# Hybrid decoder block: the bias of the softmax exponentials computed by VectorE instead of ScalarE

## Chip, cores and metric

One core of a Trainium2 chip. The metric is the device time of one launch in microseconds. Below, PE is TensorE, PEld its weight loads, DVE is VectorE, ACT is ScalarE, POOL is GpSimd, and SP is SyncE, which here only issues DMAs.

## What is computed

One decoder block on x of 1 x 2048 x 1024 in float32. The block normalises x, multiplies by a 1024 x 8192 input matrix, runs two branches, merges them by gates and ends with an output projection. One branch is a gated linear recurrence. The other, in which the change lies, is causal attention with 8 heads, each with two softmaxes whose difference weighs the values:

```
for qb in range(S // 128):                       # 16 query tiles of 128 rows
    s = einsum('bqhcd,bkhcd->bhcqk', q[q0:q1], k[:q1]) * HEAD_DIM ** -0.5      # c = 0, 1
    s = where(causal mask, s, -inf)
    p = softmax(s, axis=-1)
    w = p[:, :, 0] - lam * p[:, :, 1]
    outs.append(einsum('bhqk,bkhe->bqhe', w, v[:q1]))
o = rmsnorm(concatenate(outs), subln_g) * (1 - lam_init)
```

## The kernel before

Matrix operands are kept as a pair of float16 numbers (a high and a low part), and each product is three matmuls. The program has four stages: input transposes and first projections, the recurrence with its projections (to about 500 us), attention (about 500 to 1960 us), and the output stage.

Attention is written as 128 units, one for each head h and query tile t, with t from 0 to 15 inside a head. A unit goes through these steps:

- `a_scores`: score matmuls (L812) into the PSUM tile `sc`, of which there are two buffers. DVE copies them into the SBUF tiles `e0` and `e1` (one for each softmax) and takes row maxima into `mx` (L820; L824 for the 128 columns on the diagonal).
- `a_exp`: DVE reduces `mx` to `rm` (L835, 128 x 2, one column for each softmax). The bias `nb = -scale * rm + lsp` is 128 x 2 as well (L838). ACT then takes the exponentials of `e0` and `e1` in place (L848) with a column of `nb` as bias. Their sums go to `sm` for t of 8 and more, where a row has two pieces and so four exponentials, and directly to the chunk's tile `s0` for smaller t.
- `a_comb`, for the unit before: DVE adds the sums (L856), forms the factor `rs` (L858, L859) and combines both softmaxes (L865). ACT rounds the result to float16 (L867), POOL forms the low part (L868), and four or two transposing DMAs on SP write `pt` (L871).
- `a_pv`, three units late: the product with V (L888). Every fourth unit ends with `a_norm`: squares on ACT (L900), a chain of small DVE operations that reads `s0` (L902 to L909, L120 to L126), and the results `y`.

Between units, "fill" work is placed: the projections of the next head (k, q, v with za) and the gates gm. One fill is 24 or 48 matmuls (L192, L696) into the PSUM tile `mm` with two buffers, which ACT empties (for a gate: tanh, L713). Its weights are loaded by SP (L145, tile `wst`, two buffers, 512 KB each), squared and summed by ACT (L156, tile `jk`), rounded by DVE (`w_s`, L158), summed over partitions by PE (`tot`, L162), and scaled to float16 by ACT (L177) and DVE (L178).

The steps of a unit are written in the order `"0fc1eFp"`: scores, a fill, the combination of the unit before, further scores, exponentials, more fills, the product with V. That is not the final order. The tile framework schedules the written program with a timeline of its own, so an instruction's place on its engine's queue follows from its plan. On the chip each queue runs strictly in that order, and an instruction that waits holds up all that stands behind it.

Of the kernel before, what the change touches and what calls it, by code (L numbers as in the profile page):

```python
# [14 lines left out]
AF = mybir.ActivationFunctionType  # L15
ALU = mybir.AluOpType
# [32 lines left out]
def kernel(  # L49
# [23 lines left out]
    nc = tc.nc  # L73
# [20 lines left out]
    with ExitStack():  # L94
# [102 lines left out]
        with ExitStack() as lx:  # L197
# [351 lines left out]
            for n, (b, hf) in enumerate(seq):  # L549
# [7 lines left out]
                if n == 4:  # L557
                    mask, nlam, lsp, ciu, sub = a_consts()
# [21 lines left out]
        with ExitStack() as ax:  # L580
# [51 lines left out]
            sc_h, nsc_h, kap_h = {}, {}, {}  # L632
# [148 lines left out]
            def pieces(t):  # L781
                n = t + 1
                return [(0, min(n, 8))] + ([(8, n - 8)] if n > 8 else [])
# [46 lines left out]
            def a_exp(u):  # L830
                h, t = u.h, u.t
                nb_ = t4.tile([128, 2], F32, tag="nb", name="nb")
                if u.n > 1:
                    rm = t4.tile([128, 2], F32, tag="rm", name="rm")
                    nc.vector.tensor_reduce(out=rm, in_=u.mx[:, :, 0:u.n], axis=AX.X, op=ALU.max)  # L835
                else:
                    rm = u.mx[:, :, 0]
                nc.scalar.activation(nb_, rm, AF.Identity, scale=nsc_h[h], bias=lsp)  # L838
                if t % 4 == 0:
                    s0_t[h, t // 4] = t4.tile([128, 4, 2], F32, tag="s0", name="s0")  # L840
                u.s = s0_t[h, t // 4][:, t % 4, :]
                if t >= 8:
                    u.sm = t4.tile([128, 2, 2], F32, tag="sm", name="sm")
                pcs = pieces(t)
                for ci in range(2):
                    for pi, (b0, nb) in enumerate(pcs):
                        ev = u.e[ci, pi][1]
                        nc.scalar.activation(ev[:, 0:nb * 128], ev[:, 0:nb * 128], AF.Exp, bias=nb_[:, ci:ci + 1],  # L848
                                             scale=sc_h[h], accum_out=(u.sm[:, pi, ci:ci + 1] if t >= 8 else u.s[:, ci:ci + 1]))
# [86 lines left out]
            for i, u in enumerate(units):  # L936
                fill_to(need[u.h, u.t // 4])
                acc += per * (u.t + 1 + FB) / wsum
                nf = max(0, int(acc) - fpos[0])
                for ch in ORD:  # L940
                    if ch == "0":
                        a_scores(u, 0)
                    elif ch == "1":
                        a_scores(u, 1)
                    elif ch == "e":
                        a_exp(u)
                    elif ch == "c" and i >= 1:
                        a_comb(units[i - 1])
                    elif ch == "f" and nf > 0:
                        fill()  # L950
                        nf -= 1
                    elif ch == "F":
                        while nf > 0:
                            fill()
                            nf -= 1
                    elif ch == "p" and i >= LAG:
                        a_pv(units[i - LAG])
# [242 lines left out]
```

## Time and profile before

| | |
|---|---|
| median of 3 runs | 2519.18 us (2518.15 to 2525.44) |
| the profiled execution | 2521.62 us |
| its span | 2519.8 us, so 1.82 us lie around it |
| mean granted TensorE clock | 0.979 |
| busy share of the span | PE 93%, DVE 60%, ACT 50%, POOL 26% |
| exponentials, L848 | 384 instructions, 376.0 us on ACT |
| bias, L838 | 128 instructions on ACT, some 385 ns each |

A row of the profile names the line, the engine, the operation and its tiles (out<-in, without buffer numbers). In the view of waits, "A <- B" says that A's engine was idle until B ended. A busy PE is the bound in a stretch only where little idle time is left in it, so the stretches are looked at one by one.

### The profile page before, as it was taken

To read this page: it belongs to the slowest core of one execution; us is meant where nothing else is said; L and a number is where in the kernel's file an instruction comes from. 1 tells how busy PE (TensorE), PEld (TensorE's weight loads), DVE (VectorE), ACT (ScalarE), POOL (GpSimd) and SP (SyncE) were. 2 spreads that over 40 slices of the span, in tenths; PEclk is the share of its full clock that TensorE was granted. 3 is DMA by queue.
4 is the path that set the end of the run, shared out by engine and by line. 5 is a ranking of instruction groups with operands and counts; after the bars stand their busy time and mean duration, and the time that the engine had idled before them with its cause. 6 is when DMAs were issued, how large, how long until landed. Compare 5 with 4: busy or idle time off the path is not lost. (4 is left out here: it accounts for less than half of the span.)

```text
span 2519.8 us, 42351 instructions
## 1 busy us (share of the span) xinstructions
PE 2341.8 (93%) x15880; PEld 1298.0 (52%) x15880; DVE 1509.0 (60%) x4508; ACT 1267.7 (50%) x2284; POOL 664.1 (26%) x415
## 2 busy tenths in 40 slices
PE   5689999999998998998998998999999999999998
PEld 5344444465555654654654654645655444444443
DVE  7876767667557567567467467467476244634323
ACT  5464545566556556566466466466465344312211
POOL 2343334222222222222222122122123133323211
PEclk9899999999999999999999999999999999999999
DMA  9611111144434434335335335335335944743202
GB/s 240 103 45 34 59 42 34 51 77 102 85 75 109 86 73 107 78 70 110 77 65 112 73 73 113 71 73 114 71 70 105 280 147 136 232 154 116 86 17 101
DMA packets 511631, 243.61 MB, mean 97 GB/s; under 512 B 365385, under 2 KB 488321, under 8 KB 511425
## 3 DMA queue, kind: packets, MB, share of 16 engines
q1 hardware_dynamic: 508448, 231.56, 38.1%
q0 software_dynamic: 2816, 9.08, 1.3%
q8 instruction: 124, 2.03, 0.3%
q14 instruction: 83, 0.67, 0.1%
q10 hardware_dynamic: 160, 0.27, 0.0%
HBM read 110.79 MB, written 41.94 MB: 61 GB/s over the span
## 5 line engine op out<-in xcount | busy, mean ns | idle before, releaser
L192 PEld LDWEIGHTS <-w 128*128 128x128 f16 x5040 | 470.7, 100 | 625.1 <-issue 138.8
L192 PE MATMUL mm<-uT,w 128*128 128x512 f16 x3072 | 706.9, 386 | 28.6 <-ACT gm L713 19.5
L868 POOL TENSOR_TENSOR e<-e,e 128x1024 f16<-128x1024 f32 (+2 forms) x192 | 302.7, 1591 | 893.3 <-issue 446.0
L192 PE MATMUL ps<-uT,w 128*128 128x512 f16 (+1 forms) x1968 | 351.4, 343 | 32.3 <-ACT xr L318 21.2
L848 ACT ACTIVATE e<-e,nb,sc_h 128x1024 f32<-128x1024 f32 (+7 forms) x384 | 376.0, 980 | 7.5 <-ACT nb L838 0.4
L820 DVE TENSOR_SCALAR_CACHE_REDUCE e<-sc 128x512 f32<-128x512 f32 (+3 forms) x576 | 327.3, 597 | 79.9 <-PE sc L812 40.1
L696 PE MATMUL mm<-wva,uT 128*128 128x256 f16 x3072 | 349.3, 274 | 14.0 <-DVE w_tot L164 5.9
L1085 PE MATMUL psb<-yt,w 128*128 128x512 f16 x1536 | 334.6, 380 | 4.8 <-DMA yt<-ya_d 3.3
L696 PEld LDWEIGHTS <-uT 128*128 128x128 f16 x3072 | 298.8, 98 | 63.4 <-issue 25.2
L812 PE MATMUL sc<-K,Q 64*128 64x512 f16 (+3 forms) x1920 | 222.0, 347 | 37.7 <-DVE e L820 28.2
L1085 PEld LDWEIGHTS <-w 128*128 128x128 f16 x1536 | 149.5, 98 | 188.0 <-issue 5.6
L867 ACT ACTIVATE e<-e 128x1024 f16<-128x1024 f32 (+2 forms) x192 | 150.3, 802 | 156.2 <-DVE e L865 148.5
L888 PE MATMUL o<-V,pt 128*128 128x128 f16 x3264 | 214.5, 220 | 4.6 <-DMA pt<-e 4.6
L888 PEld LDWEIGHTS <-pt 128*128 128x128 f16 x3264 | 189.2, 98 | 55.5 <-issue 36.8
L865 DVE SCALAR_TENSOR_TENSOR e<-e,rs,e 128x1024 f32<-128x1024 f32 (+2 forms) x192 | 185.8, 995 | 2.7
L1116 PE MATMUL psf<-wo,m 128*128 128x512 f16 x720 | 155.7, 379 | 0.0
L156 ACT ACTIVATE jk<-wst 128x1024 bf16<-128x1024 f32 x80 | 84.2, 1053 | 136.6 <-DMA wst<-in_w_in_dram 101.7
L812 PEld LDWEIGHTS <-Q 64*128 64x128 f16 x1920 | 75.2, 94 | 148.5 <-issue 79.6
L838 ACT ACTIVATE nb<-rm,lsp,nsc_h 128x2 f32<-128x2 f32 x120 | 46.2, 385 | 151.3 <-DVE rm L835 151.2
L1116 PEld LDWEIGHTS <-m 128*128 128x128 f16 x768 | 75.1, 98 | 90.6
L1089 DVE SCALAR_TENSOR_TENSOR t<-gt,psb 128x512 f32<-128x512 f32 x64 | 43.9, 686 | 122.0 <-PE psb L1085 97.9
L915 POOL TENSOR_TENSOR y<-y,y 128x512 f16<-128x512 f32 x32 | 41.8, 1306 | 230.1 <-ACT y L912 219.8
(245 smaller groups left out, 2367.3 us busy)
## 6 DMA issues: line engine op xcount, KB each, us to landing
wst<-in_w_in_dram SPq DMA_DIRECT2D x64, 512.0 KB, 4.3
xt<-in_x_dram SPq DMA_DIRECT2D x32, 512.0 KB, 4.6
gm_d<-gm SPq DMA_DIRECT2D x64, 256.0 KB, 2.7
gt<-gm_d SPq DMA_DIRECT2D x32, 512.0 KB, 3.7
ya_d<-yT SPq DMA_DIRECT2D x64, 128.0 KB, 2.0
wst<-in_w_br_rnn_dram SPq DMA_DIRECT2D x16, 512.0 KB, 4.2
wst<-in_w_br_attn_dram SPq DMA_DIRECT2D x16, 512.0 KB, 4.4
wost<-in_w_out_dram SPq DMA_DIRECT2D x16, 512.0 KB, 3.6
```

The source lines that it names most:

```text
L156: nc.scalar.activation(jk, w.st, AF.Square, accum_out=ss)
L192: nc.tensor.matmul(ps, w.t[:, a, k, :], uT[:, b, k, c0:c0 + n], start=(i == 0), stop=(i == 3 * KD - 1))
L696: nc.tensor.matmul(ps[:, j, :], uT[:, a, k, s0:s0 + 128], wt[:, b, k].rearrange("p t f -> p (t f)"), start=(i == 0), stop=(i == 3 * KD - 1))
L812: nc.tensor.matmul(ps[:, ci, 0:w * 128], Q[r, a, q0:q0 + 128], K[r, b, 0:w * 128], start=(i == 0), stop=(i == 2))
L820: nc.vector.tensor_scalar(out=ev[:, 0:m], in0=ps[:, ci, 0:m], scalar1=1.0, scalar2=None, op0=ALU.mult, op1=ALU.max, accum_out=u.mx[:, ci, ...
L848: nc.scalar.activation(ev[:, 0:nb * 128], ev[:, 0:nb * 128], AF.Exp, bias=nb_[:, ci:ci + 1], scale=sc_h[h], accum_out=(u.sm[:, pi, ci:ci + ...
L865: nc.vector.scalar_tensor_tensor(out=e0[:, 0:m], in0=e1v[:, 0:m], scalar=rs, in1=e0[:, 0:m], op0=ALU.mult, op1=ALU.add)
L867: nc.scalar.activation(e1[:, 0, 0:m], e0[:, 0:m], AF.Copy)
L868: nc.gpsimd.tensor_tensor(out=e1[:, 1, 0:m], in0=e0[:, 0:m], in1=e1[:, 0, 0:m], op=ALU.subtract)
L888: nc.tensor.matmul(o, pt[:, a, kb % 8, :], V[:, kb % 4, b, :], start=(kb == 0 and i == 0), stop=(kb == n - 1 and i == 2))
L1085: nc.tensor.matmul(ps, w.t[:, p, k, :], y_t[b][:, q, k, sl], start=(i == 0), stop=(i == 3 * KD - 1))
L1116: nc.tensor.matmul(pn[n], m16[:, a, j, ms], wo[:, b, j, ns], start=(j == 0 and a == 0 and b == 0), stop=(j == KD - 1 and a == 1))
```

## The change

One instruction of `a_exp` moves from ACT to DVE. Operands and result stay as they are:

```
             else:
                 rm = u.mx[:, :, 0]
-            nc.scalar.activation(nb_, rm, AF.Identity, scale=nsc_h[h], bias=lsp)
+            nc.vector.tensor_scalar(out=nb_, in0=rm, scalar1=nsc_h[h], scalar2=lsp, op0=ALU.mult, op1=ALU.add)
             if t % 4 == 0:
                 s0_t[h, t // 4] = t4.tile([128, 4, 2], F32, tag="s0", name="s0")
```

All 128 bias instructions leave ACT's queue and stand in DVE's. The sums of the exponentials still go where they went (`s0` for t below 8). Since the framework plans the whole program anew, attention stands in another order on every engine: PE has the same instructions in 41 differing places, and SP's, ACT's and DVE's queues differ likewise. Three places show how. Numbers behind tile names tell instances apart.

ACT, in the fifth head, around 1540 us of the profile before. `jk_17396` works on a weight load, `gm_17328` empties a PSUM buffer of a fill, and `e1_17160` and `e1_17196` are the float16 results of the unit before. Before:

```order
L848 ACTIVATE e1_17196,sm_17220<-e1_17196,nb_17215,sc_h_14937 128x640
L156 ACTIVATE jk_17396,w_ss_17395<-wst_17301 128x1024
L867 ACTIVATE e1_17160<-e0_17159 128x1024
L713 ACTIVATE gm_17328<-mm_17303,w_cz_15086 128x512
L867 ACTIVATE e1_17196<-e0_17195 128x640
L838 ACTIVATE nb_17368<-rm_17369,lsp_1768,nsc_h_14938 128x2
L177 ACTIVATE wva_17389<-wst_17102,w_sg_av_17381 128x8x128
L848 ACTIVATE e0_17256,sm_17372<-e0_17256,nb_17368,sc_h_14937 128x1024
```

And now:

```order
L848 ACTIVATE e1_17196,sm_17220<-e1_17196,nb_17215,sc_h_14937 128x640
L177 ACTIVATE w16_17288<-wst_16747,w_sg_aq_17280 128x1024
L713 ACTIVATE gm_17328<-mm_17303,w_cz_15086 128x512
L867 ACTIVATE e1_17160<-e0_17159 128x1024
L867 ACTIVATE e1_17196<-e0_17195 128x640
L156 ACTIVATE jk_17396,w_ss_17395<-wst_17301 128x1024
L177 ACTIVATE wva_17389<-wst_17102,w_sg_av_17381 128x8x128
L848 ACTIVATE e0_17256,sm_17372<-e0_17256,nb_17368,sc_h_14937 128x1024
```

The gate and both float16 results stood behind the instruction that waits for a load, and now stand ahead of it. The same has happened around 799, 1354 and 1733 us.

SP, in the first two heads' overlap, around 790 us: two weight loads (`wst_7761`, `wst_7959`) among transposes of finished units. Before:

```order
L871 DMA_TRANSPOSE pt_7846<-e1_7598 128x8x128
L145 DMA wst_7761<-in_w_in_dram 128x8x128
L871 DMA_TRANSPOSE pt_7852<-e1_7715 128x4x128
L871 DMA_TRANSPOSE pt_7846<-e1_7598 128x8x128
L871 DMA_TRANSPOSE pt_7852<-e1_7715 128x4x128
L714 DMA gm_d_59<-gm_7788 128x512
L145 DMA wst_7959<-in_w_in_dram 128x8x128
L714 DMA gm_d_59<-gm_7986 128x512
```

And now:

```order
L871 DMA_TRANSPOSE pt_7846<-e1_7598 128x8x128
L871 DMA_TRANSPOSE pt_7852<-e1_7715 128x4x128
L871 DMA_TRANSPOSE pt_7846<-e1_7598 128x8x128
L871 DMA_TRANSPOSE pt_7852<-e1_7715 128x4x128
L145 DMA wst_7761<-in_w_in_dram 128x8x128
L714 DMA gm_d_59<-gm_7788 128x512
L871 DMA_TRANSPOSE pt_7996<-e1_7820 128x8x128
L145 DMA wst_7959<-in_w_in_dram 128x8x128
```

The first load stands behind three more transposes, the second behind the first transpose of the next unit. In all, 21 weight loads stand one to four rows later than before, and one earlier.

DVE, around 1358 us: `nb_15014` is a unit's bias, `s0_14865<-sm_15018` adds the sums of that unit's exponentials, and so waits for all four of them. `sc_15184` are scores of the next unit. Before:

```order
L171 SCALAR_TENSOR_TENSOR w_cz_15033<-w_iv_av_15028,cu_105 128x1
L647 TENSOR_SCALAR kap_15038<-kap_15038 128x1
L178 SCALAR_TENSOR_TENSOR wva_15035<-wst_14748,w_sg_av_15027,wva_15035 128x8x128
L164 TENSOR_SCALAR w_tot_15078<-tot_15076 128x1
L105 TENSOR_SCALAR pb_15082<-w_tot_15078 128x1
L107 TENSOR_SCALAR w_sg_agm_15080<-pb_15082 128x1
L115 TENSOR_SCALAR w_iv_agm_15081<-w_sg_agm_15080 128x1
L171 SCALAR_TENSOR_TENSOR w_cz_15086<-w_iv_agm_15081,cu_105 128x1
L820 TENSOR_SCALAR e0_15182,mx_15181<-sc_15184 128x512
L820 TENSOR_SCALAR e1_15183,mx_15181<-sc_15184 128x512
L856 TENSOR_TENSOR s0_14865<-sm_15018 128x2
```

And now:

```order
L838 TENSOR_SCALAR nb_15014<-rm_15015,nsc_h_12487,lsp_1768 128x2
L107 TENSOR_SCALAR w_sg_av_15027<-pb_15029 128x1
L115 TENSOR_SCALAR w_iv_av_15028<-w_sg_av_15027 128x1
L645 SCALAR_TENSOR_TENSOR kap_15038<-w_sg_av_15027,ciu_1773 128x1
L171 SCALAR_TENSOR_TENSOR w_cz_15033<-w_iv_av_15028,cu_105 128x1
L647 TENSOR_SCALAR kap_15038<-kap_15038 128x1
L158 CAST w_s16_15044<-w_ss_15041 128x1
L164 TENSOR_SCALAR w_tot_15078<-tot_15076 128x1
L856 TENSOR_TENSOR s0_14865<-sm_15018 128x2
L105 TENSOR_SCALAR pb_15082<-w_tot_15078 128x1
L820 TENSOR_SCALAR e0_15182,mx_15181<-sc_15184 128x512
L820 TENSOR_SCALAR e1_15183,mx_15181<-sc_15184 128x512
```

The bias has come in, and the instruction that waits for the exponentials stands ahead of the two that read the next scores and of a weight's low part (L178), where it stood behind them.

More of the change, by code (lines that the diff above doesn't have):

```diff
@@ L837, in a_exp @@
                     rm = u.mx[:, :, 0]
-                nc.scalar.activation(nb_, rm, AF.Identity, scale=nsc_h[h], bias=lsp)
+                nc.vector.tensor_scalar(out=nb_, in0=rm, scalar1=nsc_h[h], scalar2=lsp, op0=ALU.mult, op1=ALU.add)
                 if t % 4 == 0:
```

## The prediction

> **What bounds the kernel now.** I read the busy shares first, then the windows by stretch of attention, then the waits, and last the timeline around single bias instructions.
>
> ```profile
> PE 2341.8 (93%) x15880; PEld 1298.0 (52%) x15880; DVE 1509.0 (60%) x4508; ACT 1267.7 (50%) x2284; POOL 664.1 (26%) x415
> ```
>
> PE carries the span, with 178 us idle in 2519.8. ACT loses 128 x 0.385 = 49 us of its 1268, which by itself is worth nothing: ACT is half idle. Only PE's idle time can change, so I asked in which stretches of attention it lies. The windows cut each head in its first half (t below 8) and its second; a short half of four units at either end goes with these.
>
> ```profile
> core 0: us, PE busy (x) PEld busy (x) DVE busy (x) ACT busy (x) POOL busy (x), PEclk, DMA share, GB/s
> 1480.00:1600.00 120.00, 107.34 (x865) 62.68 (x864) 81.22 (x288) 75.29 (x147) 29.28 (x18) 0.96 0.49 104
> ...
> sum 870.00, PE 790.95 PEld 452.73 DVE 607.80 ACT 562.10 POOL 222.31; mean PE 98.87 PEld 56.59 DVE 75.98 ACT 70.26 POOL 27.79
> ```
>
> ```profile
> sum 590.00, PE 578.16 PEld 364.77 DVE 316.76 ACT 300.66 POOL 117.83; mean PE 72.27 PEld 45.60 DVE 39.60 ACT 37.58 POOL 14.73
> ```
>
> The first sum is that of the eight second halves, the second that of the eight first halves. In the first halves PE is idle 590.00 - 578.16 = 11.84 us in all: 64 bias instructions stand there, and nothing they do can be worth much. In the second halves it is idle 870.00 - 790.95 = 79.05 us, at a DVE load of 70% (607.80 / 870). So 64 units count. What PE waits for, from the view of waits (columns: sum of us, count, longest):
>
> ```profile
> PE sc L812 <- DVE e L820: 28.2, 26, 2.3
> PE mm L192 <- ACT gm L713: 19.5, 7, 4.0
> PE sc L812 <- DVE mx L824: 6.7, 6, 2.3
> ACT nb L838 <- DVE rm L835: 151.2, 90, 6.8
> ```
>
> In 26 + 6 = 32 places the score matmuls wait because DVE has not emptied a score buffer. Behind that lies DVE's order: it stands at an instruction that needs the exponentials (the sums L856, or the combination), and the copies of the next scores stand behind. The exponentials wait for `nb`, and `nb` for `rm`. So in 32 of 64 units the chain of bias and exponentials sets, at one remove, when PE goes on. The seven waits for `gm` are the other large item, and come from ACT's order.
>
> **The change part by part.** The durations, from the groups by shape (least/median/largest ns, first and last start):
>
> ```profile
> L838 ACT ACTIVATE nb<-rm,lsp,nsc_h x120: 371/387/390, 504.7 to 1949.9; 128x2 f32<-128x2 f32 x120
> L835 DVE TENSOR_REDUCE rm<-mx x120: 138/158/164, 504.1 to 1949.7; 128x2 f32<-128x4 f32 x32, 128x2 f32<-128x6 f32 x32, 128x2 f32<-128x8 f32 x32, 128x2 f32<-128x10 f32 x24
> L164 DVE TENSOR_SCALAR w_tot<-tot x80: 144/152/159, 12.5 to 2143.4; 128x1 f32<-128x1 f32 x80
> L120 DVE TENSOR_SCALAR rs_h<-v x32: 153/168/1655, 543.5 to 1971.9; 128x4 f32<-128x4 f32 x32
> ```
>
> 1. The chain to the exponentials. One unit, with what surrounds it on DVE and POOL (the timeline):
>
> ```profile
> 623.08 4.11 POOL L868 TENSOR_TENSOR e<-e,e 128x1024 f16<-128x1024 f32 x2 [11.55 <-issue]
> 623.76 0.15 DVE L835 TENSOR_REDUCE rm<-mx 128x2 f32<-128x10 f32 x1
> 623.84 0.15 DVE L164 TENSOR_SCALAR w_tot<-tot 128x1 f32<-128x1 f32 x1
> 623.96 0.39 ACT L838 ACTIVATE nb<-rm,lsp,nsc_h 128x2 f32<-128x2 f32 x1 [0.38 <-DVE rm L835]
> 624.44 1.24 ACT L848 ACTIVATE e<-e,nb,sc_h 128x1024 f32<-128x1024 f32 x1
> ...
> 625.77 0.14 DVE L105 TENSOR_SCALAR pb<-w_tot 128x1 int32<-128x1 int32 x1
> 625.89 1.32 DVE L120 TENSOR_SCALAR rs_h<-v 128x4 f32<-128x4 f32 x1
> ```
>
> From the end of `rm` (623.91) to the first exponential (624.44) are 0.53 us: 0.05 to reach ACT, 0.39 for `nb`, 0.09 to the next on ACT. Afterwards DVE makes `nb` right behind `rm` in some 0.16 (the median of the 128x1 rows is 0.152, of the 128x4 rows 0.168), and ACT needs 0.05 to 0.09 to start on it: 0.24. The gain is 0.29 us a unit; over 32 units -9.3 us.
>
> 2. DVE's own time. DVE gets 128 x 0.16 = 20.5 us more, half of it in the second halves. Queued behind the new instruction are the score copies L820, the sums L856 and the low parts of weights L178, and PE waits for the first. In the 32 units with a wait this is taken in full, +0.16 x 32 = +5.1 us; in the others DVE's 30% of free time covers it. Were that cover gone, it would be 64 x 0.16 = 10.2.
>
> 3. POOL beside DVE. The row of L120 above shows a price that the medians hide: the 128x4 TENSOR_SCALAR began at 625.89 inside POOL's L868, and ended at 627.21, just behind POOL's 627.19 (623.08 + 4.11): 1.32 us for 0.17. The group's largest is 1655 ns. Yet the 128x1 TENSOR_SCALARs L164 and L105 and the 128x2 TENSOR_REDUCE L835, all inside the same POOL span, took 0.14 to 0.15. The new `nb` is a TENSOR_SCALAR of 128x2, and no row shows that shape beside a working POOL. It stands behind `rm`, so the ends of `rm` tell how often it would meet one:
>
> ```profile
> 526.32 0.16 DVE L835 TENSOR_REDUCE rm<-mx 128x2 f32<-128x6 f32 x1
> 526.40 1.40 POOL L868 TENSOR_TENSOR e<-e,e 128x640 f16<-128x640 f32 x1 [7.73 <-issue]
> ...
> 1930.65 3.74 POOL L868 TENSOR_TENSOR e<-e,e 128x1024 f16<-128x1024 f32 x2 [5.38 <-issue]
> 1932.66 0.16 DVE L835 TENSOR_REDUCE rm<-mx 128x2 f32<-128x10 f32 x1
> ```
>
> These are the first and the last of 43 such meetings among 120 units with a `rm`; 30 lie in the 64 units of the second halves, and from the end of `rm` to the end of the POOL instruction there are 28.4 us in those 30, so 0.44 us a unit. The bounds: nothing, if a 128x2 behaves like the 128x1 rows; 28.4 us, if it behaves like the 128x4 rows and each unit is on the path. I take the row of 128x4 (same operation, more than one element in a row, both operands in the same memory), on the 32 units that have a wait: +0.44 x 32 = +14.2 us. It undoes the gain of point 1, since the exponentials wait with `nb`, and all of DVE's queue stands behind it.
>
> The Trainium skill, page "SBUF — State Buffer", section "Who interferes with whom", says of such a pair that a tensor_scalar can enter a mode in which DVE and GpSimd contend for one port and the loser is blocked, while a tensor_reduce never enters it on trn2. The trace agrees for L120 (1.32 us) and for L835 (0.15 us); for one element in a row it shows no block (L105, 0.14 us). By the page's rule the sum below is +3.7, by the 128x1 rows -10.5.
>
> 4. ACT's order. Four gates that stood behind a `jk` which waits for a load now stand ahead of it. One of them, about 1543 us, and PE's waits at two others, 1354 and 1733 us:
>
> ```profile
> 1540.51 0.39 SPq L145 DMA_DIRECT2D wst<-in_w_in_dram  x1
> 1544.42 1.06 ACT L156 ACTIVATE jk<-wst 128x1024 bf16<-128x1024 f32 x1 [4.13 <-DMA wst<-in_w_in_dram]
> 1546.42 0.67 ACT L713 ACTIVATE gm<-mm,w_cz 128x512 f32<-128x512 f32 x1
> 1547.14 2.29 PE L192 MATMUL mm<-uT,w 128*128 128x512 f16 x5 [3.96 <-ACT gm L713]
> ...
> 1357.70 4.57 PE L192 MATMUL mm<-uT,w 128*128 128x512 f16 x14 [3.93 <-ACT gm L713]
> ...
> 1736.00 2.29 PE L192 MATMUL mm<-uT,w 128*128 128x512 f16 x5 [2.78 <-ACT gm L713]
> ```
>
> PE stood 3.96 us; with the gate ahead of the wait (4.13 on ACT), some 0.8 remain for the weight's scaling L177 that comes ahead instead: -3.2. The same at 1354 us (3.93, so -3.0) and at 1733 us (2.78, so -1.9). At the fourth, 799 us, a second cause is added:
>
> ```profile
> 791.08 4.45 SPq L871 DMA_TRANSPOSE pt<-e  x3
> 796.26 0.38 SPq L145 DMA_DIRECT2D wst<-in_w_in_dram  x1
> 797.26 1.04 ACT L156 ACTIVATE jk<-wst 128x1024 bf16<-128x1024 f32 x1
> 801.55 1.06 ACT L156 ACTIVATE jk<-wst 128x1024 bf16<-128x1024 f32 x1 [3.17 <-DMA wst<-in_w_in_dram]
> 803.33 0.38 PE L192 MATMUL mm<-uT,w 128*128 128x512 f16 x1 [3.82 <-ACT gm L713]
> ```
>
> The load that feeds the first `jk` is now issued behind the three transposes of 791.08 (4.45 us of SP's queue), and the gate stands behind that `jk`: the first wait takes over from the second and is larger, +1.8. In sum -3.2 - 3.0 - 1.9 + 1.8 = -6.3 us.
>
> 5. The other moved loads. 20 more weight loads stand one to four rows later on SP. A transpose there takes some 1.5 us of the queue (4.45 / 3), so a load may come 1.5 to 6 us later. It lands 4.3 us after its issue, by the page's median:
>
> ```profile
> wst<-in_w_in_dram SPq DMA_DIRECT2D x64, 512.0 KB, 4.3
> ```
>
> I followed each to its `jk`: most had landed 4 to 130 us before it was read, so I put them at nothing; that cover is what rival three takes away. The moved sums L856 at 1358 us, now ahead of the next score copies, are of the same kind: they cost what the wait for the exponentials lasts longer than before, and elsewhere the order moves the other way; nothing for the balance.
>
> The sum: -9.3 + 5.1 + 14.2 - 6.3 + 0 = **+3.7 us**. The profiled execution took 2521.62 us (span 2519.8 and 1.82 around it), so 2525.3 on its basis. It stands 2.44 above the median of the runs shown, 2519.18, and against that median I expect 2522.9, so 2523 us.
>
> **The rivals.** The first, faster: POOL doesn't hold a 128x2, which then goes like L164 and L105. The sum is -9.3 + 5.1 - 6.3 = -10.5, so 2508.7 us. For it: three instructions of up to two elements a row that ran in 0.15 inside POOL's time. Against it: two of them have a single element, and the third is another operation.
>
> The second, slower: DVE becomes the pace of all units in the second halves. Each unit then pays -0.29 + 0.16 + 0.44 = +0.31, and it decides once 45 of the 64 are on the path ((7.6 + 6.3) / 0.31, where 7.6 is 0.3% of the time), against 32 now. With 64: 64 x (-0.13) + 28.4 = +20.1, less the 6.3 of the gates: +13.8, 2533 us. For it: the held DVE also holds the copies L820, so new waits for `sc` appear where there were none. Against it: at 70% load DVE regains a delay of 0.4 in the next idle time.
>
> The third, slower: the delayed loads hurt as at 799 in seven heads, 1.8 each, +12.6, and the gates gain nothing because another load's `jk` stands ahead. Then -9.3 + 5.1 + 14.2 + 12.6 = +22.6, about 2542 us. For it: 21 loads moved, and ACT's queue holds all behind a `jk` that waits. Against it: the slack of all but a few.
>
> **How the numbers follow.** What a measurement of this kernel tells from no change is about 0.3%, 7.6 us: 2511.6 to 2526.8 counts as the same. The likeliest case (the sum as it stands) gets 0.42, and its own range, with 7.6 either way in the gates and the waits, is 2515 to 2531. The first rival gets 0.22, the second 0.26, the third 0.10. Low end: the first rival with all four gates gaining (-9.3 + 5.1 - 8.1 = -12.3): 2507. High end: point 3's full bound, all 64 units and no gain at the gates, +20.1: 2539. That leaves out most of the third rival and the tail of the first. Faster 0.22 is the first rival, slower 0.36 the second and third, same 0.42 the sum.
>
> **What the profile after would show.** Point 1: ACT's first exponential some 0.24 us behind the end of `rm` where no POOL instruction runs. Point 3: the group of L838, now on DVE, with a median near 0.16 and a largest above 1.5 us, ending with POOL's instructions; if its largest is 0.17, the first rival holds. Point 2: waits `sc` <- L820 near 28 us plus 10 or so in sum; far more, with PE idle near 100 us in the second halves, is the second rival. Point 4: waits `mm` <- `gm` down from 19.5 to about 13. Point 5: no new waits for `wst` at the `jk` ahead of a fill. I am wrong if the idle time in the second halves moves by something other than these: an order in which PE meets a wait that no row of before shows.

## The result, and the profile after

The changed kernel takes 2536.65 us (median of 5, 2532.16 to 2539.50), against 2519.18 before: a ratio of 1.0069, 95% interval 1.0057 to 1.0081. It is slower by 17.5 us. The time lies inside the stated range, near its upper end; the likeliest case, no change that can be measured, did not come. The profiled execution took 2539.5 us.

The busy times after, from the page:

```profile
PE 2356.0 (93%) x15880; PEld 1303.0 (51%) x15880; DVE 1562.9 (62%) x4636; ACT 1222.9 (48%) x2156; POOL 672.6 (27%) x415
```

The windows of attention (span of the window, then PE, PEld, DVE, ACT and POOL, granted clock, DMA), first of the kernel before and then of the changed one, each window from the same matmuls to the same matmuls:

```profile
500.00:1960.00 1460.00, 1369.11 (x10924) 817.49 (x10922) 924.57 (x3393) 862.75 (x1804) 340.14 (x224) 0.98 0.41 88
```

```profile
500.00:1979.00 1479.00, 1379.76 (x10917) 822.31 (x10915) 978.00 (x3521) 819.20 (x1675) 349.80 (x223) 0.98 0.41 86
```

Attention takes 19 us more. PE does the same work in it, but its idle time goes from 90.89 to 99.24 us, and its busy time up by 10.65. Since no matmul was added, the second part is a slower PE: the mean clock of the execution was 0.974, where it was 0.979 before. The same eight second halves of the heads as in the prediction, at the places to which they have moved (by their edges these windows hold 6302 matmuls, the prediction's 6277):

```profile
sum 898.00, PE 810.86 PEld 461.69 DVE 637.29 ACT 540.03 POOL 233.42; mean PE 101.36 PEld 57.71 DVE 79.66 ACT 67.50 POOL 29.18
```

Idle time is 87.14 us here, 79.05 before. DVE's load rose by one point, 637.29 / 898 = 71%. PE's waits, and the waits of ACT and DVE on which the rest turns, after:

```profile
DVE s L856 <- ACT e L848: 133.8, 53, 5.1
DVE rs L858 <- ACT e L848: 56.0, 47, 2.5
ACT jk L156 <- DMA wst<-in_w_in_dram: 115.9, 37, 9.9
PE sc L812 <- DVE e L820: 50.0, 40, 3.6
PE sc L812 <- DVE mx L824: 8.3, 6, 2.2
PE mm L192 <- ACT gm L713: 3.6, 4, 2.3
```

and the three of these that were not shown of before:

```profile
DVE s L856 <- ACT e L848: 108.9, 42, 5.6
DVE rs L858 <- ACT e L848: 73.4, 46, 3.6
ACT jk L156 <- DMA wst<-in_w_in_dram: 101.7, 33, 8.6
```

The gates came free, from 19.5 to 3.6 us. The scores pay for it, from 28.2 to 50.0. Behind them DVE's sums L856, of the units with t of 8 and more, wait 25 us longer for the exponentials, and ACT 14 us longer for weight loads. (In the units with smaller t, where L858 reads the exponentials' sums directly, DVE waits 17 us less: 56.0 where it was 73.4.)

One place shows how these hang together. It is the fourth of the gates, 1733 us of the profile before (times are starts, then durations; the bracket is the idle time and what ended it). Before:

```profile
1729.27 0.38 SPq L145 DMA_DIRECT2D wst<-in_w_in_dram  x1
...
1733.28 1.06 ACT L156 ACTIVATE jk<-wst 128x1024 bf16<-128x1024 f32 x1 [2.00 <-DMA wst<-in_w_in_dram]
...
1735.28 0.67 ACT L713 ACTIVATE gm<-mm,w_cz 128x512 f32<-128x512 f32 x1
1735.40 5.62 SPq L871 DMA_TRANSPOSE pt<-e  x4
...
1738.29 1.23 ACT L848 ACTIVATE e<-e,nb,sc_h 128x1024 f32<-128x1024 f32 x1
...
1745.27 0.15 DVE L856 TENSOR_TENSOR s<-sm 128x2 f32<-128x2 f32 x1
```

and after:

```profile
1746.46 1.23 SPq L871 DMA_TRANSPOSE pt<-e  x1
1746.57 4.05 POOL L868 TENSOR_TENSOR e<-e,e 128x1024 f16<-128x1024 f32 x2 [19.14 <-issue]
1746.97 0.67 ACT L713 ACTIVATE gm<-mm,w_cz 128x512 f32<-128x512 f32 x1
1747.69 4.48 PE L192 MATMUL mm<-uT,w 128*128 128x512 f16 x20 [0.29 <-ACT gm L713]
1747.80 0.52 SPq L145 DMA_DIRECT2D wst<-in_w_in_dram  x1
...
1749.58 1.07 DVE L838 TENSOR_SCALAR nb<-rm,nsc_h,lsp 128x2 f32<-128x2 f32 x1
...
1753.04 1.06 ACT L156 ACTIVATE jk<-wst 128x1024 bf16<-128x1024 f32 x1 [5.40 <-DMA wst<-in_w_in_dram]
...
1754.10 1.23 ACT L848 ACTIVATE e<-e,nb,sc_h 128x1024 f32<-128x1024 f32 x1
...
1758.69 0.16 DVE L856 TENSOR_TENSOR s<-sm 128x2 f32<-128x2 f32 x1 [3.05 <-ACT e L848]
1758.77 0.69 DVE L820 TENSOR_SCALAR_CACHE_REDUCE e<-sc 128x512 f32<-128x512 f32 x1
...
1760.13 1.15 PE L812 MATMUL sc<-K,Q 64*128 64x384 f16 x6 [3.09 <-DVE e L820]
```

Before, the load is issued ahead of the unit's transposes, its `jk` waits 2.00 us, and the gate stands behind it; the exponentials come later and wait for nothing. After, the load stands behind the first transpose of a unit that has just been rounded. The gate goes early (PE waits 0.29 for it instead of 2.78). But `jk` now waits 5.40 us, and the exponentials stand behind `jk`: `nb` is there at 1750.65 (1749.58 + 1.07), and the first exponential starts at 1754.10. DVE's sums wait for the last one, the score copies stand behind the sums, and PE waits 3.09. Here the wait was not taken away; it went from the gate to the exponentials. The row of `nb` shows in passing what was expected of POOL: it ends at 1750.65, where POOL's 4.05 from 1746.57 end at 1750.62.

### The profile page after: what moved, and what is told of

It reads as the page before. It is cut to its first block, busy times and chain, and to the rows that moved or that the text cites. A ratio compares the mean times of both kernels' runs of the same rounds, so it can differ in the third digit from the quotient of the medians.

```text
span 2537.7 us, 42361 instructions
## 1 busy us (share of the span) xinstructions
PE 2356.0 (93%) x15880; PEld 1303.0 (51%) x15880; DVE 1562.9 (62%) x4636; ACT 1222.9 (48%) x2156; POOL 672.6 (27%) x415
## 5 line engine op out<-in xcount | busy, mean ns | idle before, releaser
L868 POOL TENSOR_TENSOR e<-e,e 128x1024 f16<-128x1024 f32 (+2 forms) x192 | 310.8, 1632 | 957.1 <-ACT e L867 501.9
L820 DVE TENSOR_SCALAR_CACHE_REDUCE e<-sc 128x512 f32<-128x512 f32 (+3 forms) x576 | 327.3, 596 | 49.4 <-DMA pt<-e 26.2
L812 PE MATMUL sc<-K,Q 64*128 64x512 f16 (+3 forms) x1920 | 227.1, 352 | 63.1 <-DVE e L820 50.0
L156 ACT ACTIVATE jk<-wst 128x1024 bf16<-128x1024 f32 x80 | 84.2, 1053 | 150.5 <-DMA wst<-in_w_in_dram 115.9
L856 DVE TENSOR_TENSOR s<-sm 128x2 f32<-128x2 f32 x64 | 10.2, 160 | 133.8 <-ACT e L848 133.8
```

The lines of the kernel that those rows point to most:

```text
L156: nc.scalar.activation(jk, w.st, AF.Square, accum_out=ss)
L812: nc.tensor.matmul(ps[:, ci, 0:w * 128], Q[r, a, q0:q0 + 128], K[r, b, 0:w * 128], start=(i == 0), stop=(i == 2))
L820: nc.vector.tensor_scalar(out=ev[:, 0:m], in0=ps[:, ci, 0:m], scalar1=1.0, scalar2=None, op0=ALU.mult, op1=ALU.max, accum_out=u.mx[:, ci, ...
L868: nc.gpsimd.tensor_tensor(out=e1[:, 1, 0:m], in0=e0[:, 0:m], in1=e1[:, 0, 0:m], op=ALU.subtract)
```

## The experiments

An instruction of the program has the same number in both kernels, since the change adds and removes none. So the order of each queue can be written down as a list of numbers and imposed on either kernel; the framework then plans nothing:

```
+    for eng, seq in json.loads(...).items():          # for each engine its instruction numbers, in order
+        prev = None
+        for n in seq:
+            i = by.get(n)
...
+            if prev is not None:
+                tc.add_manual_dep(i, prev.name, info, reason="pin_order")
+            prev = i
```

**The order and the engine, each alone.** First, the kernel before (bias on ACT) in the order of the changed kernel:

> The bias stays on ACT, in front of the unit's first exponential; every other instruction of all five queues stands in the order that the changed kernel has (queue orders pinned). Theory A, the moved instruction costs the time (longer on DVE, held by POOL): this order alone brings the gates forward and takes no hold, so some 6 us under the kernel before, about 2513 us, with the waits of a fill for its gate down from 19.5 to about 4 us and the waits of the scores for L820 near 28 us. Theory B, the new order costs it: about 2533 to 2537 us, with the waits of the scores for L820 near 50 us as in the changed kernel. Theory C, both half: about 2527 us.

Measured: 2537.63 us, ratio 1.0074 (1.0061 to 1.0086): the whole loss, without the change. PE's and ACT's waits in it:

```profile
PE sc L812 <- DVE e L820: 46.8, 36, 3.6
PE mm L192 <- ACT gm L713: 7.1, 4, 3.4
...
ACT jk L156 <- DMA wst<-in_w_in_dram: 117.6, 35, 8.8
```

Then the changed line in the order of before:

> The bias on DVE, right behind its row maximum; every other instruction of all five queues stands in the order of the kernel before (pinned). Theory A: all of the loss and the gates' gain taken away from it, so about 2519 + 17 + 12 = 2548 us or somewhat less, waits of the scores for L820 at 50 us or more, the gates' waits near 19 us as before. Theory B: about 2519 us, within 0.3%. Theory C: about 2530 us.

Measured: 2523.54 us, ratio 1.0019 (1.0009 to 1.0029), 4 us slower, and PE waits no more than before:

```profile
PE sc L812 <- DVE e L820: 28.2, 25, 2.4
...
PE mm L192 <- ACT gm L713: 18.2, 7, 4.2
```

Theory B holds. What the diff says costs some 4 us (2 to 7 by the interval) of the 17.5; what the planner made of it costs the rest.

**What POOL costs the moved bias.** Both orders as before, L868 cut to one column:

```
-                    nc.gpsimd.tensor_tensor(out=e1[:, 1, 0:m], in0=e0[:, 0:m], in1=e1[:, 0, 0:m], op=ALU.subtract)
+                    nc.gpsimd.tensor_tensor(out=e1[:, 1, 0:1], in0=e0[:, 0:1], in1=e1[:, 0, 0:1], op=ALU.subtract)
...
-                        nc.sync.dma_start_transpose(out=pt[:, hl_, 0:nb, :], in_=e1[:, hl_, 0:m])
+                        nc.sync.dma_start_transpose(out=pt[:, hl_, 0:nb, :], in_=e1[:, 0, 0:m])
```

With the bias on DVE:

> As the one before (bias on DVE, order of the kernel before), but POOL's L868 works on one column instead of 128 to 1024, and the second transpose of a unit reads the high part in its place (the low part of the weights is left out). To be read against the same cut with the bias on ACT. If the hold by POOL is what the moved bias costs, it comes within 5 us of that kernel, either side, and L838 has no row above 0.35 us. If its own 0.29 us on DVE's queue is the cost, the difference is as large as between the uncut two (10 us or more).

and on ACT:

> The kernel before in its own order with the same cut of L868 (one column, the second transpose reads the high part). It shows what POOL's part costs by itself: other DVE instructions held by it (L124, L125, L171, L178 and L904, some 40 us over the span) go free, most of it off PE's path, so 0 to 10 us under the kernel before.

Measured: 2491.80 us (ratio 0.9890, 0.9876 to 0.9903) and 2493.98 us (0.9906, 0.9892 to 0.9919). With POOL out of the way the bias on DVE is 2 to 4 us better than on ACT, inside the intervals; with POOL there it is 4 us worse. So the hold is worth 6 to 9 us, with some 5 us of uncertainty either way. L838 in the changed kernel, then in the order of before, then with L868 cut (least, median and largest ns):

```profile
L838 DVE TENSOR_SCALAR nb<-rm,nsc_h,lsp x120: 270/288/2098, 504.0 to 1967.5; 128x2 f32<-128x2 f32 x120
```

```profile
L838 DVE TENSOR_SCALAR nb<-rm,nsc_h,lsp x120: 287/289/2100, 498.8 to 1951.8; 128x2 f32<-128x2 f32 x120
```

```profile
L838 DVE TENSOR_SCALAR nb<-rm,nsc_h,lsp x120: 287/289/1956, 498.9 to 1916.0; 128x2 f32<-128x2 f32 x120
```

In the last one a single instruction is far above 0.3 us, which the expectation had excluded; it met POOL's work for the stage after:

```profile
1890.46 1.96 DVE L838 TENSOR_SCALAR nb<-rm,nsc_h,lsp 128x2 f32<-128x2 f32 x1
1890.49 1.90 POOL L150 TENSOR_TENSOR wst<-wst,wfac_r 128x1024 f32<-128x1024 f32 x1 [1.66 <-DMA wst<-in_w_br_rnn_dram]
```
The size of the cut itself was not expected: some 26 us with the bias on ACT, where 0 to 10 were expected. It frees the other DVE instructions that POOL held, and lets the transposes start earlier; this pair does not tell the two apart.

**Which queue's order costs it.** Bias on ACT, and the order of the changed kernel for some queues only:

> Bias on ACT; TensorE's queue alone in the order of the changed kernel, the four other queues in the order of the kernel before. Theory S (the loads that SP issues later hold ACT, and with it the exponentials, DVE's sums and the next score copies): nothing of the loss, 2519 us within 0.3%. Theory P (the matmuls of a fill moved to other places among the scores leave PE without cover): about 2530 us or more. Theory D (DVE's sums stand ahead of the next score copies): about 2519 us.

> Bias on ACT; the queues of DVE and ACT in the order of the changed kernel, PE, SP and POOL as before. Theory S: the gates' gain alone, about 2512 us. Theory P: the same. Theory D: most of the loss, about 2530 us or more, waits of the scores for L820 above 40 us.

> Bias on ACT; PE, DVE, ACT and POOL in the order of the changed kernel, SP alone in the order of before: each weight load stands where it stood among the transposes. Theory S: the loss is gone and the gates' gain is left, 2512 to 2519 us, and ACT's waits of L156 for wst fall from 57 us in attention to 43 or less. Theories P and D: 2530 us or more, as with all queues moved (2537.6).

> Bias on ACT; DVE, ACT, SP and POOL in the order of the changed kernel, PE alone in the order of before. Theory S: the whole loss, about 2537 us. Theory P: the loss is gone, 2512 to 2519 us. Theory D: about 2530 us or more.

Measured, with the two corners:

| queues in the new order | us | ratio |
|---|---|---|
| none (before), measured beside these | 2519.8 to 2522.1 | 1 |
| PE | 2534.05 | 1.0046 (1.0034 to 1.0059) |
| DVE, ACT | 2590.69 | 1.0277 (1.0261 to 1.0294) |
| PE, DVE, ACT, POOL | 2549.91 | 1.0112 (1.0096 to 1.0129) |
| DVE, ACT, SP, POOL | 2589.62 | 1.0265 (1.0251 to 1.0279) |
| all five | 2537.63 | 1.0074 (1.0061 to 1.0086) |

None of the three theories comes through. Theory S falls in the form in which it was put: with SP's order of before put back the kernel is slower, not faster. Its waits:

```profile
ACT jk L156 <- DMA wst<-in_w_in_dram: 116.4, 37, 8.7
PE sc L812 <- DVE e L820: 45.6, 36, 3.2
```

ACT waits as long as with all queues moved (117.6), so putting the loads back among the transposes did not by itself shorten that wait. PE's order alone costs 12 us, but by the starts of equal matmuls its profiled execution loses 16 us at one place, the end of the first head, and nothing after; with all queues moved the loss grows by 1 to 4 us in each head. It is a misfit of its own. The queues' orders fit each other, and none of them can be priced alone.

**ACT's waits for the loads.** So the wait itself was taken away, in both orders:

```
-            nc.scalar.activation(jk, w.st, AF.Square, accum_out=ss)
+            if w.tag[0] == "a":
+                nc.scalar.activation(jk, uT[:, 0, :, 0:w.n], AF.Square, scale=p2(-11), accum_out=ss)
+            else:
+                nc.scalar.activation(jk, w.st, AF.Square, accum_out=ss)
```

> Bias on ACT, all queues in the order of the changed kernel. The sums of squares of attention's weights (L156) read an array that has long been in SBUF instead of the load just made, so ACT never waits there for a load (the true norm of these weights is left out); the scalings L177 and L178 still read the load. To be read against the same cut in the order of before. Theory S2 (in its own order the loss is ACT waiting at L156 for late loads, with the exponentials behind it): the two come within 5 us of each other, some 10 to 25 us under 2519. Theory O (the loss is spread over the order and not in those waits): this one stays 12 us or more above the other.

> The same cut of L156 in the order of the kernel before. It takes away 43 us of ACT's waits in attention, and with them most of the 19.5 us in which a fill waits for its gate: some 10 to 20 us under the kernel before, 2500 to 2510 us, by either theory.

Measured: 2499.14 us in the new order (ratio 0.9915, 0.9901 to 0.9928), 2493.62 in the old (0.9897, 0.9881 to 0.9912). The orders are 5.5 us apart where they were 17.8: some two thirds of the order's loss go with ACT's waits at L156. The interval of the 5.5 reaches from about 0 to 10, so it may be less than half or nearly all, and Theory S2 is supported and not sharp. PE's idle time speaks for the smaller share: from the first score matmul to the last product with V it is 93.6 us before and 105.1 with the order alone, and with the cut still 72.6 and 79.8. What stays is seen in PE's waits (line numbers are 3 higher here), new order first:

```profile
PE sc L815 <- DVE e L823: 37.6, 38, 3.6
```

```profile
PE sc L815 <- DVE e L823: 24.5, 26, 2.3
```

Of the 18.6 us by which the order alone lengthens the waits for the score copies (28.2 to 46.8), 13 remain though ACT no longer waits for those loads, and 6 us of the gates' waits go the other way (6.7 to 0.4). Where these 13 come from, perhaps DVE's sums ahead of the copies, was not separated further.

**Shorter POOL instructions.** The bias on DVE, order of before, and

```
-                    nc.gpsimd.tensor_tensor(out=e1[:, 1, 0:m], in0=e0[:, 0:m], in1=e1[:, 0, 0:m], op=ALU.subtract)
+                    lo = [nc.gpsimd.tensor_tensor(out=e1[:, 1, x:min(x + 256, m)], in0=e0[:, x:min(x + 256, m)],
+                                                  in1=e1[:, 0, x:min(x + 256, m)], op=ALU.subtract).ins.name
+                          for x in range(0, m, 256)]
```

> Bias on DVE, all queues in the order of before, and POOL's L868 in pieces of 256 columns instead of up to 1024: nothing is left out. If DVE is held for one POOL instruction at a time, the hold falls from up to 2.1 us to at most some 0.75 us, L838 has no row above 1.0 us, and it comes to about 2510 us: a part of the 32 us by which the cut to one column was faster (2491.8 against 2523.5). If that gain came from the transposes' earlier start and not from the hold, or POOL's pieces follow each other without a gap for DVE, it stays at 2523 us or goes above.

Measured: 2517.05 us, ratio 0.9975 (0.9965 to 0.9984), against 1.0019 unsplit: 0.44%, some 11 us. The largest L838 is 0.773 us, as a hold by one POOL instruction at a time would have it:

```profile
L838 DVE TENSOR_SCALAR nb<-rm,nsc_h,lsp x120: 287/289/773, 503.1 to 1943.2; 128x2 f32<-128x2 f32 x120
```

What the pieces gain with the bias on ACT was not run, so how much of this needs the moved bias stays open.

**A version that beats both.** The same, and on ACT's queue the `jk` that waited moved behind what was ready, at nine places. At the place before 1543 us:

```
-L156 jk<-wst
 L713 gm<-mm
 L867 e1
 L867 e1
+L156 jk<-wst
```

> Nothing left out. Bias on DVE, the order of before, L868 in pieces of 256 columns as in the run before, and on ACT's queue nine of the L156 that waited for a load moved behind what stood ready behind them: five gates L713, six of the roundings L867 and three exponentials L848. If ACT's waits at L156 delay PE as the cut of L156 showed (25 to 30 us in all), a good part of the gates' 18 us comes back: about 2505 us, waits of a fill for its gate down from 18 to 8 us or less. If the wait only moves to the next instruction, 2517 us as without it.

Measured: 2508.59 us, ratio 0.9945 (0.9931 to 0.9959): 13 us under the kernel before and 28 under the changed one. PE's waits in it:

```profile
PE sc L812 <- DVE e L820: 41.6, 35, 3.8
...
PE mm L192 <- ACT gm L713: 2.0, 3, 0.9
```

The gates' wait has gone (18.2 to 2.0 us), but the waits for the score copies rose by as much, from 24.9 us with the pieces alone:

```profile
PE sc L812 <- DVE e L820: 24.9, 23, 2.9
```

The gain against that run is 0.30%, 7.6 us, and it is not idle time: from the first score matmul to the last product with V PE idles 88.9 us here and 87.0 there. Its busy time fell, from 1398.2 to 1392.8 us, at a higher clock (the mean of the runs is 0.981 here, 0.979 there). The last section shows a likely reason: the gates' long waits had been followed by stretches at half clock.

## Why the prediction was right and wrong

The range held the time, but by a mixture of errors, so that it held is in good part luck; the sum's sign came out right and its parts did not.

1. **The chain** was to fall from 0.53 to 0.24 us. In units where nothing holds `nb` it is 0.42 (median from the end of `rm` to the exponential, in the order of before). The price of `nb` was taken from rows whose scalars are constants; it reads two operands of one element a row, and takes 0.289. A row of before would have said so, the 128x4 with one such operand, 0.224 on average where the 128x4 with a constant has a median of 0.168:

```profile
L902 DVE TENSOR_SCALAR v<-s,kap 128x4 f32<-128x4 f32 x32 | 7.2, 224 | 9.8 <-ACT e L848 9.8
```

So -9.3 was -0.11 x 32 = -3.5 us.

2. **DVE's own time** is 0.289 and not 0.16. Nothing of it shows in PE's waits: in the order of before those for L820 are 28.2 us with the bias on either engine. The cover that the prediction granted to half of the units was there for all.

3. **POOL's hold** is real, and the row of 128x4 was the right one to go by; the first rival falls. The sum of all L838 beyond their undisturbed time in the changed kernel is 60.6 + 4.7 - 128 x 0.289 = 28.3 us:

```profile
L838 DVE TENSOR_SCALAR nb<-rm,nsc_h,lsp 128x2 f32<-128x2 f32 x120 | 60.6, 505 | 2.5
L838 DVE TENSOR_SCALAR nb<-mx,nsc_h,lsp 128x2 f32<-128x2 f32 x8 | 4.7, 582 | 0.0
```

Its effect was 6 to 9 us and not 14.2, by the runs with L868 cut, and by the profiles mostly through the clock (last section): from the first score matmul to the last product with V, PE's idle time is 90.2 us with the bias on DVE in the order of before and 93.6 in the kernel before, its busy time 1407.0 and 1395.7. The Trainium skill, page "SBUF — State Buffer", section "Who interferes with whom", calls the loser fully blocked for the whole instruction of the other; the trace agrees, with an `nb` that ends 0.03 us behind POOL's pair, and a largest hold that falls from 2.1 to 0.77 us with POOL's pieces.

4. **ACT's order** was to bring the gates' waits from 19.5 to about 13; it brought them to 3.6.

5. **The moved loads and sums, put at nothing: this is the step that failed.** It was taken load by load, by the slack that each had in the order of before. In the new order something else stands behind `jk`: at the place shown the exponentials, where it had been the gate. The wait of `jk` grew by some 14 us in all, and DVE's sums waited 25 us longer for the exponentials. Point 4 counted the gain of that exchange, and point 5 left out what it cost. The order by itself was put at -6.3 and is +17.8 us. The cut of L156 supports `jk` as a cause of a part of this; the rest, the 13 us of waits for the score copies above all, stays open. In the profile of the order alone attention is 17 us longer (1477 where it was 1460), 12 of them idle time of PE and 5 a slower PE, and for the clock the prediction had no term. The third rival had the loads' lateness, but with the gates as what suffers; it had the smallest of the four chances, 0.10. The second rival has the waits that the profile after shows, `sc` at 50.0, but not their cause: they stand there with the bias on ACT too (46.8).

The parts add up to a little more than the whole: 17.8 for the order and 3.8 for the engine, 17.5 for both. (In the low end of the range the -8.1 for all four gates is the sum of three; nothing above turns on it.)

## To carry to other kernels

Where a scheduler orders the program, a one-line change is two changes; pin the queues' orders and time each alone before believing either. An instruction that waits for a load on an in-order queue moves its wait to whatever stands behind it: look at what that is in the new order before counting a gain. Long POOL instructions such as L868 are worth cutting into pieces where they hold small work of DVE; that was measured here with the bias on DVE only. And a few long waits of PE can cost more than many short ones of the same sum, as the next section shows.

## What was not expected of the hardware

The clock took a part of its own. The trace's clock records show TensorE at half its clock in pieces of 3.41 us, and at full clock otherwise: 13 such pieces in attention before, 20 after, 19 with the order alone, 14 with L868 in pieces and 10 in the last version. With the bias on DVE in the order of before PE idles less in the second halves (75 us between equal matmuls, where the kernel before has 80) and still the kernel is slower: 23 pieces in its profile, and a mean clock of 0.9747 over 11 runs, where 15 runs of the kernel before on the same chip have 0.9776. 0.0029 of PE's 2342 us are 7 us. The Trainium skill, page "TensorE: Matmul & The Clock Gate", section "Part 1: The HAM clock gate", has the gate half or full only, decided in free-running windows of 3413 ns by how busy PE was; the two levels and the length agree with the records here. The prediction had no term for it.

What stands ahead of such a piece can be read from the same records. Cut attention (500 to 1950 us) into windows of 3.41 us that begin where the pieces begin, and take PE's idle time in each. In the profiles of before, after, the order alone and the engine alone, 53 windows at full clock are followed by one at half clock, and in each of the 53 PE had idled 1.81 us or more. Among all other windows at full clock only 3 had as much. So in these profiles the lower clock follows idle time crowded into one window, over half of it, and not the sum of the waits. The engine alone has 15 windows with that much, where the kernel before has 11, though it idles less in all; why its waits crowd more was not separated. With L868 in pieces, five stretches at half clock, 7 of the 14 pieces, begin behind a window whose longest wait was one for a gate (1.6 to 3.4 us of it); in the last version none does.
